# A hybrid decoder block on one core: operands three products ahead, residual loads among the merges, and three smaller moves

## The chip, the cores and the metric

The kernel runs on one core of a Trainium2 chip. TensorE (PE) multiplies, VectorE (DVE), ScalarE (ACT) and GpSimd (POOL) do the elementwise work, and SyncE (SP) issues most DMAs. The metric is the device time of one execution in microseconds (us); lower is better.

## The reference

One layer over 1024 tokens of width 1024, all in float32:

```
h = x + 1/2 * SwiGLU_1(rms(x))                      # hidden width 2816
u = rms(h);  [q | k | v | p | gate_logits] = u @ W_in
A: causal dilated window attention, 12 heads in 3 groups   -> @ W_A
B: causal means over 2/4/8/16 positions, 4 channel groups  -> @ W_B
h = h + (sigmoid(gA) * yA + sigmoid(gB) * yB) @ W_o
h = h + 1/2 * SwiGLU_2(rms(h))
out = rms_final(h)
```

## The kernel before

All products are in float32 split into two parts, a rounded high part and the rest, the lower part. A product of two such operands takes three matmuls (high times high, high times lower, lower times high; `three`). ScalarE makes the high part by a copy (L303), and VectorE or GpSimd makes the lower part by a subtraction (L306): VectorE for every third operand (`n_lo % 3`), GpSimd for the others.

The large products are done by a scheme of Strassen's kind with seven products instead of eight. In the projections a `Quad` is one block of 128 output columns with the products m = 1 to 7 in the order `ORDER = (1, 6, 2, 7, 5, 4, 3)`. Each is 12 matmuls of 128x512. `operand(m)` makes the weights' operand: for m = 6 it takes two sums on VectorE (L345, L347), for 7 and 3 one (L351, L356), and the rest take a piece or a sum that is there already. The operands lie in tiles of tag "wc", four of them. `run(m)` does the product into a PSUM bank; products 2 and 3 add onto the banks of 1 and 5. So the result of 5 (`out(5)`) has to be read before product 3 may begin. There are four PSUM banks of tag "mm" (products 1, 2, 5, 3) and four of tag "acc".

Most of the program is in stretches that are issued in the order in which they are written (`manual_schedule`): each engine takes its own instructions in that order and waits where one is not ready. These places matter here:

- `up` does the first half of a SwiGLU. For the column pairs that were begun early, a list `items` gives the products, and iteration k issues the operand of product k + 2, product k, and then the result of product k - 1 (`a_out`, `b_out`; L487 is `a_out(5)`).
- The input projection has 19 quads (`MIX`: three groups of q and k and of v, then pool and gate blocks) and does the same with `mix_operand`, `quad.run` and `Mix.out` (L982 to L999; L993 is `out(5)`). The first four quads have their products 1 and 2 done beforehand. The result of product 1 goes ahead of the operand. A list `later` holds jobs that go on by one step an iteration, behind the result: transposes of v (`turn`, L1058 to L1061), pool windows and their matmuls (`window`, L1078 to L1102), and `split_late`, which splits weights for later stages and stores them.
- The merges, 16 of them, come after attention. Merge k multiplies the attention parts (`att_parts`, four tiles of tag "h") with W_A into an "mm" bank (L1701), VectorE multiplies with the gate (L1703), GpSimd adds the pool branch (L1707), and SP is told to load the input of merge k + 5. The first eight do the first half of the tokens, the others the second; all of them read the four tiles of `att_parts`.
- The product with W_o goes by `step_o(i)`, i = 0 to 13, two steps for each of seven products; a step is four groups of six matmuls (`multiply_o`, L1884), one bank each. Products alternate between the "acc" and the "mm" banks. `sum_o` makes sums of merges on GpSimd, `split_o` the parts of the left operand (L1867 on ScalarE, `o_lo`, L1871, on VectorE), `load_whole` and `split_whole` the parts of single W_o blocks (L1381, L1408, L1411), `load_w_o` loads blocks that were split earlier (L1377), and `adds_o` adds a finished bank onto the residual h (L1890, L1892). `reload(t)` takes a new tile of tag "h" (there are eight) and loads the residual's rows of tile t into it (L1830), on SP's queue. Steps 0 and 1 stand among the merges.
- At the end `store_last` scales the last four row tiles and stores them; the last one goes in two halves on two queues.

A tile that is taken while all of its tag are in use makes the first instruction that writes it wait for the last reader of an old one; for a load this wait is at its place in the issuing engine's queue.

Of the kernel before, what the change touches and what calls it, by code (L numbers as in the profile page):

```python
# [13 lines left out]
OP = mybir.AluOpType  # L14
# [4 lines left out]
D = 1024  # L19
NT = S // P  # L20
# [98 lines left out]
def three(hi_lo_l, hi_lo_r):  # L119

    lh, ll = hi_lo_l
    rh, rl = hi_lo_r
    return ((lh, rh), (lh, rl), (ll, rh))
# [3 lines left out]
def tile_block(  # L127
# [28 lines left out]
    nc = tc.nc  # L156
# [31 lines left out]
    h = []  # L188
# [66 lines left out]
    inv = {}  # L255
# [10 lines left out]
    def scaled(t, out, gain):  # L266
        ve.scalar_tensor_tensor(out, h[t], inv.pop(t)[:, 1:2], gain, op0=OP.mult, op1=OP.mult)
# [119 lines left out]
    class Entry:  # L387
# [13 lines left out]
        def out(self, i):  # L401
            self.todo[i][2](self.todo[i][1], self.banks.pop(i))
# [152 lines left out]
    def up(sv, sums, between, name, room, begun):  # L555

        with tc.manual_schedule():
            last = ORDER[-1]  # L560
            items = [(q, w, m, out) for q in begun for w, out in ((q.A, q.a_out), (q.B, q.b_out))
                     for m in ORDER if m not in (1, 2)]
            then = Pair(sv, len(begun), sums)
            ahead = [(w, m) for _, w, m, _ in items] + [(then.A, m) for m in ORDER[:2]]
            parts, res = [], []
            for k, (q, w, m, out) in enumerate(items):
                ahead[k + 2][0].operand(ahead[k + 2][1])
                res.append(w.run(m))
                if m == last:
                    raws.depth = 6 if q is not begun[-1] else 4  # L570
                if k > 0:
                    p, _, m, out = items[k - 1]
                    out(m, res[k - 1])
                    for g in parts:
                        next(g, None)
                    if p is not q:
                        parts.append(p.parts())
            out = items[-1][3]
            out(last, res[-1])
            for g in parts:  # L580
                for _ in g:
                    pass
            begun[-1].finish()
        for j in range(len(begun), NPAIR - 1):
            q, then = then or Pair(sv, j, sums), None
            for m in ORDER:
                q.a(m)
            if j == NPAIR - 2:
                between()
            for m in ORDER[:-2]:  # L590
                q.b(m)
            if j == NPAIR - 2:
                end = Pair(sv, NPAIR - 1, sums)
                for m in ORDER[:2]:
                    end.A.operand(m)
            for m in ORDER[-2:]:
                q.b(m)
            q.finish()
        d = Down(name, sums, sv.half_tile, end)
        with tc.manual_schedule():  # L600
            items = [(w, m, out) for w, out in ((end.A, end.a_out), (end.B, end.b_out)) for m in ORDER]
            n = len(items)
            res = []
            for k, (w, m, out) in enumerate(items):
                if k + 2 < n:
                    items[k + 2][0].operand(items[k + 2][1])
                if k == 7:
                    d.load(0, tmp)
                    d.load(1, row)
                if k == n - 4:  # L610
                    d.sums_w(0)
                if k == n - 2:
                    raws.back(2)
                    d.sums_w(1)
                res.append(w.run(m, k < n - 1))
                if k == n - 1:
                    d.dp = room()
                    d.load(2)
                    d.begin(0)
                if k > 0:  # L620
                    items[k - 1][2](items[k - 1][1], res[k - 1])
            d.begin(1)
            end.b_out(ORDER[-1], res[-1])
        return d
# [583 lines left out]
    def mix_operand(k):  # L1208
        if k < len(items):
            q, m = items[k]  # L1210
            if q == len(mixes):
                mixes.append(Mix(svm, q))
            mixes[q].quad.operand(m, None if k > 1 else gp)
# [96 lines left out]
    with tc.manual_schedule():  # L1310
        entry.run(high_mix, after_mix)

        later, results = [], {}
        load_table(0)
        for k in range(len(items) + 4):
            if k - 1 in results and items[k - 1][1] == 1:
                mixes[items[k - 1][0]].out(1, results.pop(k - 1))
            mix_operand(k + 2)
            if k - 2 in range(len(items)):
                mixes[items[k - 2][0]].activate()  # L1320
            if k < len(items):
                q, m = items[k]
                results[k] = mixes[q].quad.run(m)
                if m == 7 and q < len(LATE):
                    later.append([k + 1, split_late(q)])
            if k - 1 in results:
                q, m = items[k - 1]
                mixes[q].out(m, results.pop(k - 1))
                if m == 3:
                    later.append([k, mixes[q].finish()])  # L1330
            for job in list(later):
                if job[0] <= k:
                    wait = next(job[1], 0)
                    job[0] = k + wait
                    if not wait:
                        later.remove(job)
            if k == 7 * 6:
                load_pool_w()
            if k == 7 * 12:
                tables.clear()  # L1340
                mask = keep.tile([P, 384], F32, tag="gain", bufs=1, name="mask")
                nc.sync.dma_start(mask, c_mask)
            if k == len(items) - 12:
                later.append([k, first_ring()])
            if k == len(items) - 7:
                load_pool(2)
                load_pool(3)
            if k == len(items) - 5:
                load_pool(0)
                load_pool(1)  # L1350
            if k == len(items) - 4:
                load_branch(0)
                load_values(0, row_part)
# [384 lines left out]
    with tc.manual_schedule():  # L1738
# [50 lines left out]
        q = N // 2  # L1789
# [83 lines left out]
    def split_o(i):  # L1873
        hi_o(i)
        lo_o(i)

    def multiply_o(i, t):
        m, st = divmod(i, 2)
        if m not in banks:
            banks[m] = [bank(("acc", "mm")[m % 2], f"wo{m}_{q}") for q in range(4)]  # L1880
        w, ts = w_o_parts[i], slice(t * P, (t + 1) * P)
        for j in range(2):
            for q, (l, r) in enumerate(three(tuple(v[:, j, ts] for v in ops[i]), tuple(w[:, v, j] for v in range(2)))):
                pe.matmul(banks[m][t], l, r, start=(st == 0 and j == 0 and q == 0), stop=(st == 1 and j == 1 and q == 2))  # L1884

    def add_o(m, t):
        for (th, n), sign in DOWN[m].to:
# [6 lines left out]
    def step_o(i, ts=range(4)):  # L1894
        for t in ts:
            multiply_o(i, t)
        if 3 in ts and (i + 3) // 2 in (2, 3, 4, 6) and i + 3 < STEPS:
            load_w_o(i + 3)

    def adds_o(m, ts):  # L1900
        for t in ts:
            add_o(m, t)
# [11 lines left out]
    with tc.manual_schedule():  # L1914
# [12 lines left out]
        for k in range(6, 11):  # L1927
            merge(k)
            if k in (7, 9):
                load_whole(2 + (k - 7) // 2)  # L1930
            if k == 8:
                sum_o(3)
                split_o(2)
        step_o(1)
        sum_o(4)
        split_o(3)
        for k in range(11, 16):
            merge(k)
            if k in (12, 14):
                split_whole(2 + (k - 12) // 2, ve)  # L1940
        for t in range(4, NT):
            reload(t)
        X2.update(sums_of_x(late["xa"], "f2", ("b21", "b11")))
        for i in range(2, STEPS - 4):
            step_o(i)
            m, st = i // 2 - 1, i % 2
            adds_o(m, range(2 * st, 2 * st + 2))
            if i in (6, 7):
                load_whole(i + 4)
            if i == 6:  # L1950
                ac.activation(warm, mhalf, AF.Silu)
            sum_o(i + 3)
            split_o(i + 2)
            if i in (8, 9):
                split_whole(i + 2, ve)

# [94 lines left out]
    def store_last(t):  # L2051
        rows = slice(t * P, (t + 1) * P)
        y = ends[t]
        if t < NT - 1:
            scaled(t, y, final_gain)
            nc.sync.dma_start(out[rows, :], y)
            return
        st = inv[t]
        ac.activation(y[:, LOWS], y[:, LOWS], AF.Copy, scale=st[:, 1:2])
        nc.scalar.dma_start(out[rows, LOWS], y[:, LOWS])  # L2060
        ve.scalar_tensor_tensor(y[:, HIGHS], h[t][:, HIGHS], st[:, 1:2], final_gain[:, HIGHS], op0=OP.mult, op1=OP.mult)
        nc.sync.dma_start(out[rows, HIGHS], y[:, HIGHS])
# [124 lines left out]
```

## Time and profile before

| | |
|---|---|
| median of 3 runs | 1917.43 us (1917.08 to 1917.56) |
| profiled execution | 1919.57 us |
| its span, first to last instruction | 1917.8 us |
| TensorE busy | 1900.8 us, 99% |
| VectorE busy | 1346.2 us, 70% |
| ScalarE, GpSimd busy | 760.0 and 733.5 us |
| granted TensorE clock | 0.999 |

A row of the waits reads: who waited, its line, for whom; us in total, number of times, the longest. A row of a timeline reads: start and duration in us, engine, line, operation, tile written <- tiles read, shapes, count, and in brackets the idle time before it and what ended it. PEld is TensorE's loading of weights, which overlaps its matmuls. In names of tiles, buffer numbers are left out: `u_mixm` is a bank of the input projection, `wc_mixm` an operand of it, `y_m` a result.

### The profile page before, as it was taken

Reading aid. Unit: us, or ns where it says so; the run is one execution under the profiler, and the core shown is the slowest. Engines: PE = TensorE matmul, PEld = TensorE weight load, DVE = VectorE, ACT = ScalarE, POOL = GpSimd, SP = SyncE. Lnnn points to the kernel's source line nnn. Section 1 sums busy time; section 2 is a strip of 40 time slices with the busy share of each in tenths; the row PEclk is TensorE's granted clock in tenths of the full one; section 3 lists DMA queues with packets and bytes.
Section 4 is the critical chain, followed back from the end, with each engine's and each line's share of the span. In section 5 each row is a group of like instructions: output and inputs, shape, how many; then the busy total and the mean of one; then the engine's idle time right before and its main releaser. Section 6 shows DMA issues by size and latency. Waiting matters only on the chain. (4 is left out here: it accounts for less than half of the span.)

```text
span 1917.8 us, 24914 instructions
## 1 busy us (share of the span) xinstructions
PE 1900.8 (99%) x8938; PEld 1575.5 (82%) x8938; DVE 1346.2 (70%) x2016; ACT 760.0 (40%) x1364; POOL 733.5 (38%) x548
## 2 busy tenths in 40 slices
PE   9999999999999999999999999999999999999998
PEld 7888888888888888888877888788888888888886
DVE  7886556657776776668875896788665556577777
ACT  6333333333344543334444762253333333333344
POOL 5433333331222365545544455553333333312132
PEclk9999999999999999999999999999999999999999
DMA  4154223336466627665567967643434223454564
GB/s 188 47 195 173 86 88 105 137 109 214 149 236 214 203 94 245 228 217 202 207 247 277 308 213 264 240 167 113 179 104 137 83 88 105 159 185 145 195 216 165
DMA packets 144796, 331.98 MB, mean 173 GB/s; under 512 B 19104, under 2 KB 39840, under 8 KB 143136
## 3 DMA queue, kind: packets, MB, share of 16 engines
q1 hardware_dynamic: 137136, 308.00, 46.1%
q10 hardware_dynamic: 7536, 22.39, 3.4%
q8 instruction: 70, 1.15, 0.2%
q14 instruction: 54, 0.44, 0.1%
HBM read 229.61 MB, written 100.73 MB: 172 GB/s over the span
## 5 line engine op out<-in xcount | busy, mean ns | idle before, releaser
L714 PE MATMUL d_f<-bhi_f,ahi_f 128*128 128x512 f32 x616 | 240.4, 390 | 0.0
L714 PE MATMUL d_f<-bhi_f,alo_f 128*128 128x512 f32 x616 | 239.7, 389 | 0.0
L714 PE MATMUL d_f<-blo_f,ahi_f 128*128 128x512 f32 x616 | 239.6, 389 | 0.0
L314 PE MATMUL u_mixm<-xhi_t_mix,wc_mixm 128*128 128x512 f32 x608 | 195.2, 391 | 1.1 <-POOL wc_mixm L306 1.0
L676 POOL TENSOR_TENSOR alo_f<-g_f,ahi_f 128x512 fp32r<-128x512 f32 x60 | 84.4, 1422 | 291.8 <-ACT ahi_f L672 291.8
L314 PE MATMUL u_mixm<-xhi_b_mix,wc_mixm 128*128 128x512 f32 x456 | 149.0, 392 | 0.3 <-DVE y_m L993 0.3
L714 PEld LDWEIGHTS d_f<-bhi_f,alo_f 128*128 128x128 f32 x616 | 115.6, 188 | 24.1
L714 PEld LDWEIGHTS d_f<-bhi_f,ahi_f 128*128 128x128 f32 x616 | 115.6, 188 | 24.0 <-DVE xlo_b_mix L385 0.2
L314 PEld LDWEIGHTS u_mixm<-xhi_t_mix,wc_mixm 128*128 128x128 f32 x608 | 113.8, 188 | 26.2 <-POOL wc_mixm L306 2.7
L714 PEld LDWEIGHTS d_f<-blo_f,ahi_f 128*128 128x128 f32 x616 | 115.7, 188 | 23.8
L314 PE MATMUL u_mixm<-xlo_t_mix,wc_mixm 128*128 128x512 f32 x304 | 118.4, 389 | 0.0
L306 POOL TENSOR_TENSOR wc_mixm<-s_mixm,wc_mixm 128x512 fp32r<-128x512 f32 x52 | 74.0, 1425 | 100.4 <-ACT wc_mixm L303 96.4
L314 PEld LDWEIGHTS u_mixm<-xhi_b_mix,wc_mixm 128*128 128x128 f32 x456 | 85.6, 188 | 18.3 <-issue 0.7
L303 ACT ACTIVATE wc_mixm<-s_mixm 128x512 fp32r<-128x512 f32 x76 | 47.5, 629 | 126.7 <-DVE s_mixm L347 67.4
L314 PE MATMUL u_mixm<-xlo_b_mix,wc_mixm 128*128 128x512 f32 x228 | 88.8, 389 | 0.0
L672 ACT ACTIVATE ahi_f<-g_f 128x1024 fp32r<-128x1024 f32 x84 | 81.9, 975 | 3.6 <-DMA g_f<-gs_f 3.6
L306 POOL TENSOR_TENSOR wc_mixm<-raw,wc_mixm 128x512 fp32r<-128x512 f32 x40 | 60.6, 1519 | 45.0 <-ACT wc_mixm L303 38.1
L672 ACT ACTIVATE bhi_f<-s_f2w 128x512 fp32r<-128x512 f32 x55 | 32.7, 627 | 94.4 <-DVE s_f2w L692 84.3
L1884 PE MATMUL wo<-w_o,o_hi 128*128 128x512 f32 x224 | 69.5, 391 | 0.2 <-issue 0.2
L314 PEld LDWEIGHTS u_mixm<-xlo_t_mix,wc_mixm 128*128 128x128 f32 x304 | 57.1, 188 | 11.7
L672 ACT ACTIVATE bhi_f<-s_f1w 128x512 fp32r<-128x512 f32 x55 | 32.9, 630 | 82.7 <-DVE s_f1w L692 77.8
L676 DVE TENSOR_TENSOR alo_f<-g_f,ahi_f 128x1024 fp32r<-128x1024 f32 (+1 forms) x48 | 58.7, 1223 | 7.7 <-ACT ahi_f L672 7.7
(1312 smaller groups left out, 5106.7 us busy)
## 6 DMA issues: line engine op xcount, KB each, us to landing
g_f<-gs_f SPq DMA_DIRECT2D x70, 512.0 KB, 4.7
gs_f<-y_f SPq DMA_DIRECT2D x88, 256.0 KB, 2.9
raw<-in_w2a_dram SPq DMA_DIRECT2D x35, 512.0 KB, 3.3
raw<-in_w2b_dram SPq DMA_DIRECT2D x35, 512.0 KB, 3.3
gs_f<-gb_f SPq DMA_DIRECT2D x46, 256.0 KB, 2.3
raw<-in_w1a_dram SPq DMA_DIRECT2D x22, 512.0 KB, 5.6
raw<-in_w3a_dram SPq DMA_DIRECT2D x22, 512.0 KB, 5.6
raw<-in_w1b_dram SPq DMA_DIRECT2D x22, 512.0 KB, 4.2
```

Source lines behind the costliest of these rows:

```text
L303: ac.activation(w[:, 0], src, AF.Copy)
L306: eng.tensor_tensor(w[:, 1], src, w[:, 0].bitcast(F32), op=OP.subtract)
L314: pe.matmul(p, a, b, start=(start and k == 0 and q == 0), stop=(k == 3 and q == 2), skip_group_check=not start)
L672: ac.activation(hi[:, c], src, AF.Copy)
L676: eng.tensor_tensor(lo[:, d], src[:, o], hi[:, d].bitcast(F32), op=OP.subtract)
L714: pe.matmul(self.banks[m][t], l, r, start=(first and q == 0), stop=(last and q == 2))
L1884: pe.matmul(banks[m][t], l, r, start=(st == 0 and j == 0 and q == 0), stop=(st == 1 and j == 1 and q == 2))
```

## The change

Five edits. The fifth result is issued ahead of the operand in `up`. In the input projection the operand of product k + 3 instead of k + 2 is issued in iteration k, and `split_late` begins one iteration earlier. In `multiply_o` the matmuls with the lower part of the left operand come last of the six. `reload(4)` and `reload(5)` move from behind the merges to behind merges 8 and 9, and at i = 2 `split_o(4)` moves ahead of the adds. The last store but one is scaled and stored in two halves.

```diff
@@ up
             for k, (q, w, m, out) in enumerate(items):
+                soon = k > 0 and items[k - 1][2] == 5
+                if soon:
+                    items[k - 1][3](5, res[k - 1])
                 ahead[k + 2][0].operand(ahead[k + 2][1])
...
                     p, _, m, out = items[k - 1]
-                    out(m, res[k - 1])
+                    if not soon:
+                        out(m, res[k - 1])
@@ the input projection's loop
-            mix_operand(k + 2)
+            if k == 0:
+                mix_operand(2)
+            mix_operand(k + 3)
...
                 if m == 7 and q < len(LATE):
-                    later.append([k + 1, split_late(q)])
+                    later.append([k, split_late(q)])
@@ multiply_o
-        for j in range(2):
-            for q, (l, r) in enumerate(three(tuple(v[:, j, ts] for v in ops[i]), tuple(w[:, v, j] for v in range(2)))):
-                pe.matmul(banks[m][t], l, r, start=(st == 0 and j == 0 and q == 0), stop=(st == 1 and j == 1 and q == 2))
+        for n, (q, j) in enumerate((q, j) for qs in ((0, 1), (2,)) for j in range(2) for q in qs):
+            l, r = three(tuple(v[:, j, ts] for v in ops[i]), tuple(w[:, v, j] for v in range(2)))[q]
+            pe.matmul(banks[m][t], l, r, start=(st == 0 and n == 0), stop=(st == 1 and n == 5))
@@ the merges and steps
             if k == 8:
                 sum_o(3)
                 split_o(2)
+                reload(4)
+            if k == 9:
+                reload(5)
...
-        for t in range(4, NT):
+        for t in range(6, NT):
             reload(t)
...
             m, st = i // 2 - 1, i % 2
+            if i == 2:
+                split_o(i + 2)
             adds_o(m, range(2 * st, 2 * st + 2))
...
             sum_o(i + 3)
-            split_o(i + 2)
+            if i > 2:
+                split_o(i + 2)
@@ store_last
         if t < NT - 1:
-            scaled(t, y, final_gain)
-            nc.sync.dma_start(out[rows, :], y)
+            st = inv.pop(t)
+            for c in (LOWS, HIGHS) if t == NT - 2 else (slice(0, D),):
+                ve.scalar_tensor_tensor(y[:, c], h[t][:, c], st[:, 1:2], final_gain[:, c], op0=OP.mult, op1=OP.mult)
+                nc.sync.dma_start(out[rows, c], y[:, c])
             return
```

## The prediction

> **What bounds the kernel now.** I read the page's busy shares first, then the waits of TensorE (the matmuls' and the weight loads') by stretches, then the timelines of the places that they name.
>
> ```profile
> PE 1900.8 (99%) x8938; PEld 1575.5 (82%) x8938; DVE 1346.2 (70%) x2016; ACT 760.0 (40%) x1364; POOL 733.5 (38%) x548
> PE wo L1884 <- DVE o_lo L1871: 1.9, 2, 1.7
> PE u_mixm L314 <- POOL wc_mixm L306: 1.0, 2, 0.6
> PE u_f21a L314 <- DVE y_f L487: 0.5, 1, 0.5
> PEld u_mixm L314 <- POOL wc_mixm L306: 2.7, 4, 1.1
> PEld wo L1884 <- DVE o_lo L1871: 2.8, 2, 2.1
> ```
>
> TensorE is busy for 1900.8 of 1917.8 us, so nothing that another engine does counts unless a matmul waits for it. The change alters neither the number nor the shape of the matmuls. What it can win is the few waits listed; what it can lose is any new wait. All working below is therefore a list of waits of TensorE, gone and new. The matmul rows undercount a wait, since the modelled end of a matmul overruns the start of the next; the weight-load rows overcount it a little. One place calibrates both:
>
> ```profile
> 1193.02 6.96 PE L1701 MATMUL ya<-att,ya 128*128 128x512 f32 x30
> 1211.07 0.70 PE L1884 MATMUL wo<-w_o,o_hi 128*128 128x512 f32 x2 [0.15 <-issue]
> 1213.44 0.50 PE L1884 MATMUL wo<-w_o,o_lo 128*128 128x512 f32 x1 [1.67 <-DVE o_lo L1871]
> ```
>
> Thirty matmuls in 6.96 us, the last one 0.39 long, start every (6.96 - 0.39) / 29 = 0.227 us. Two matmuls from 1211.07 make the third due at 1211.52; it started at 1213.44, so 1.92 us were lost where one row says 1.67 and the other 2.1. I add 0.25 to a matmul row or take 0.2 from a weight-load row.
>
> **Waits that the change removes.** The fifth result first (`up`): m = 3 adds onto the bank of m = 5, so it waits until `a_out(5)` (L487) has read that bank. VectorE reaches that read behind the operand of the product after next:
>
> ```profile
> 1338.15 0.68 DVE L345 TENSOR_TENSOR s_f21b<-raw 128x512 f32<-128x512 f32 x1
> 1338.87 0.69 DVE L347 TENSOR_TENSOR s_f21b<-s_f21b,raw 128x512 f32<-128x512 f32 x1
> 1339.67 0.63 ACT L303 ACTIVATE wc_f21b<-s_f21b 128x512 fp32r<-128x512 f32 x1 [3.36 <-DVE s_f21b L347]
> 1340.34 0.69 DVE L306 TENSOR_TENSOR wc_f21b<-s_f21b,wc_f21b 128x512 fp32r<-128x512 f32 x1 [0.78 <-ACT wc_f21b L303]
> 1340.95 0.68 DVE L487 TENSOR_TENSOR y_f<-u_f21a,y_f 128x512 f32<-128x512 f32 x1
> 1341.78 0.47 PE L314 MATMUL u_f21a<-xhi_b_f,wc_f21a 128*128 128x512 f32 x1 [0.52 <-DVE y_f L487]
> ```
>
> Moved ahead of the two sums, the read no longer waits for them: 0.52 + 0.25 = 0.75 us gone. The operand comes 0.7 us later and has a whole product (12 x 0.227 = 2.72 us) to spare. The other started pairs show no such wait, so nothing is counted for them.
>
> Operands three ahead: the four waits for a lower part by GpSimd sum to 2.7 - 4 x 0.2 = 1.9 us, bounds 1.0 and 2.7. A lead of one more product covers the longest (1.1), so I count 1.9 us gone.
>
> Lower parts last, and `split_o(4)` ahead of the adds: the two waits for `o_lo` are 2.8 - 2 x 0.2 = 2.4 us, and the pair at 1211.07 started 0.3 after it was due (its bank was still being added, below). The low parts are now wanted two matmuls (0.45 us) later, and at i = 2 they no longer stand behind three adds. I count 2.7 us gone, bounds 1.9 and 3.3.
>
> The last store but one by halves:
>
> ```profile
> 1911.33 1.28 DVE L267 SCALAR_TENSOR_TENSOR hn_n<-h_last,nst,gain_final 128x1024 f32<-128x1024 f32 x1
> 1913.06 0.75 DVE L2061 SCALAR_TENSOR_TENSOR hn_last<-h_last,nst_last,gain_final 128x512 f32<-128x512 f32 x1 [0.44 <-POOL nst_last L2088]
> ```
>
> Its first half is ready after about 0.7 us instead of 1.28, so its transfer starts some 0.6 us earlier and is out of the way of the very last one. Two halves cost VectorE 0.2 us more, inside the 0.44 that L2061 waits anyway. Between 0 and 0.6; I take 0.3. Sum removed: 0.75 + 1.9 + 2.7 + 0.3 = 5.65 us.
>
> **What operands three ahead add.** In iteration k the operand of product k + 3 now stands ahead of the result of k - 1. Where k - 1 is the fifth product of a quad, k + 3 is the sixth of the next quad (the order is 1, 6, 2, 7, 5, 4, 3): the operand with two sums, L345 and L347. That is just the order which cost `up` its wait, and `Mix.out(5)` (L993) is not moved ahead here. Each third operand gets its lower part from VectorE (`n_lo % 3`); counted through the list, the sixth is among them for the quads after 3, 6, 9, 12 and 15 (behind quads 0 to 2 the sums fall a product earlier, since the next quad has only five products left). Where VectorE is free, the sums run while product five is still on TensorE and cost nothing: over the run it is busy 70% of the time. But in some quads a job of the iteration before holds VectorE until after product five has ended, by waiting for transposes or pool matmuls that TensorE does behind product five. These are its rows for the fifth result, and the third product's start:
>
> ```profile
> 803.23 0.69 DVE L1061 TENSOR_TENSOR v<-tv,v 128x512 fp32r<-128x512 f32 x1 [3.10 <-ACT v L1060]
> 744.29 0.68 DVE L993 TENSOR_TENSOR y_m<-u_mixm,y_m 128x512 f32<-128x512 f32 x1
> 745.61 0.39 PE L314 MATMUL u_mixm<-xhi_b_mix,wc_mixm 128*128 128x512 f32 x1
> 803.83 0.68 DVE L993 TENSOR_TENSOR y_m<-u_mixm,y_m 128x512 f32<-128x512 f32 x1
> 805.52 0.48 PE L314 MATMUL u_mixm<-xhi_b_mix,wc_mixm 128*128 128x512 f32 x1
> 862.89 0.68 DVE L993 TENSOR_TENSOR y_m<-u_mixm,y_m 128x512 f32<-128x512 f32 x1
> 864.58 0.48 PE L314 MATMUL u_mixm<-xhi_b_mix,wc_mixm 128*128 128x512 f32 x1
> 923.00 0.68 DVE L993 TENSOR_TENSOR y_m<-u_mixm,y_m 128x512 f32<-128x512 f32 x1
> 924.75 0.39 PE L314 MATMUL u_mixm<-xhi_b_mix,wc_mixm 128*128 128x512 f32 x1
> 962.44 0.68 DVE L993 TENSOR_TENSOR y_m<-u_mixm,y_m 128x512 f32<-128x512 f32 x1
> 964.19 0.39 PE L314 MATMUL u_mixm<-xhi_b_mix,wc_mixm 128*128 128x512 f32 x1
> 1004.06 0.68 DVE L306 TENSOR_TENSOR wc_mixm<-raw,wc_mixm 128x512 fp32r<-128x512 f32 x1
> 1005.48 0.47 PE L314 MATMUL u_mixm<-xhi_b_mix,wc_mixm 128*128 128x512 f32 x1 [0.32 <-DVE y_m L993]
> ```
>
> They are quads 3, 6, 9, 12, 14 and 16; the first row is the job that held VectorE in quad 6, and L993 began as it ended. In `up` the stretch from the start of the first sum to the start of the third product is 1341.78 - 1338.15 = 3.63 us. Put where L993 begins now, it makes the third product start at 747.92, 807.46, 866.52 and 926.63: 2.31, 1.94, 1.94 and 1.88 us late, 8.1 in all. Where GpSimd makes the lower part, the stretch is two sums and the read, 1.41 + 0.83 = 2.24 us: quad 14 would start it at 962.44 + 2.24 = 964.68, 0.5 late, and quad 16, where L306 moves ahead and the sums take its place, at 1004.06 + 2.24 = 1006.30, 0.8 late. New waits: 9.4 us. From below: none, if the sums get in ahead of the job; from above 3 more, if a weight load that the first sum needs is not there a product earlier. I take 9.4, as each term comes from a row of the same order of the same instructions.
>
> [...]
>
> **What the residual loads add.** `reload` takes a tile of tag "h", of which there are 8. Beside merge 8 all are in use: four hold `att_parts`, which every merge to the last reads, and four hold h[0] to h[3]. So `reload(4)` waits for a tile that TensorE gives back only in merge 15, and it waits at the head of SP's queue, ahead of the loads of merge 14, of `load_whole(3)` and of merge 15:
>
> ```profile
> 1192.95 0.32 SPq L1686 DMA_DIRECT2D merge<-gate  x1
> 1195.22 0.38 SPq L1381 DMA_DIRECT2D w_o_in<-in_w_o_dram  x1
> 1199.95 0.32 SPq L1686 DMA_DIRECT2D merge<-gate  x1
> 1201.31 2.08 SPq L1830 DMA_DIRECT2D h_again<-h_dram  x4
> 1199.72 1.06 ACT L1408 ACTIVATE w_o<-w_o_in 128x1024 fp32r<-128x1024 f32 x1 [2.91 <-DMA w_o_in<-in_w_o_dram]
> 1200.82 1.44 DVE L1411 TENSOR_TENSOR w_o<-w_o_in,w_o 128x1024 fp32r<-128x1024 f32 x1 [0.85 <-ACT w_o L1408]
> 1203.10 0.69 DVE L1703 TENSOR_TENSOR merge<-merge,ya 128x512 f32<-128x512 f32 x1 [0.85 <-DMA merge<-gate]
> 1203.90 0.44 PE L1884 MATMUL wo<-w_o,o_hi 128*128 128x512 f32 x1
> 1210.28 1.29 DVE L1890 TENSOR_TENSOR h_again<-wo,h_again 128x512 f32<-128x512 f32 x2 [5.89 <-DMA h_again<-h_dram]
> GB/s 0 0 0 49 82 115 229 221 311 385 344 320 393 287 377 262 393 393 328 393 393 393 328 393 377 344 426 377 426 410 426 393 426 442 377 442 410 410 442 393
> ```
>
> Merge 15 ends at 1193.02 + 6.96 = 1199.98; the first tile is free after its second matmul, about 1199.3. From there SP issues reload(4), merge 14, whole(3), reload(5), merge 15, 0.5 MB each. The GB/s row (0.25 us a slice from 1199.95, a queue that had run dry) moves 1.05 MB in 4.5 us, 1.57 in 5.9 and 2.62 in 8.5. So merge 14 lands at 1203.8, whole(3) at 1205.2, merge 15 at 1207.8. TensorE does not need these loads for the merges, but the third and the fourth product of `step_o(2)` take over the "mm" banks of merges 14 and 15, and the fourth started at 1203.90, right behind merge 15's multiply (1203.10 + 0.69). VectorE's new order: merge 14 to 1204.5, the lower part of w_o(3) to 1205.2 + 1.06 + 1.44 = 1207.7, merge 15 to 1208.5. The fourth product starts at 1208.6, 4.7 us late. Landings can lag the bytes: reload(4), behind 1.5 MB, would by this row have landed 7.1 us after 1199.95 and was there at 1210.28, 3.2 us more. Bounds 4.7 and 7.9; I take 5.2, near the lower one, since VectorE took the multiply at 1203.10 just as the row has its bytes done (0.55 MB). With that, reload(4) is long there when the adds come.
>
> [...]
>
> **Sum.** -5.65 + 9.4 + 5.2 = +9.0 us. The profiled execution took 1919.57 us (span 1917.8, and 1.8 around it) and would take 1928.6; the median of the runs, 1917.43, lies 2.1 below it, and on it the sum is 1926.4 us. By itself this case runs from 1921.5 (only half of the projection's terms) to 1930.
>
> **Rivals.** (a) Faster: the written order does not bind, because the framework's queues let the reload and the operands stand where they hold up nothing. Then all is gain, 1917.43 - 5.65 = 1911.8. It decides if the fifth result stays within 1.0 us of where it was in quads 6, 9 and 12 and SP does not stop after merge 13. For it: the slack of the fifth result is above 1 us in most quads. Against: L993 behind L1061 and L487 behind L306 are in the written order. (b) The sums get in ahead of the held job, and only SP's stop costs: -5.65 + 5.2 = -0.45, 1917.0. Against: the job is written into the iteration before. (c) A tile is free for reload(4) and only the projection pays: -5.65 + 9.4, 1921.2. Against: 4 + 4 tiles of 8. (d) Worse: landings lag by 3.2 us, and weights come late for the sums: +2.7 + 3, about 1932.
>
> **How the numbers follow.** The main case has 0.66, (a) 0.11, (b) 0.10, (c) 0.08, (d) 0.05. A measurement of this kernel can tell about 0.2%, 3.8 us, from no change: (a) is faster; (b), (c) and a little of the main case are the same; the rest is slower. The range 1916.5 to 1930.5 leaves out (a) and (d), 0.16.
>
> **What would show it.** Right: the matmul waits for `u_mixm` on L993's successor rise from 0.3 to some 9 us in about six places, with the sums ahead of it on VectorE; the waits for GpSimd's lower parts, for `o_lo` and for L487 are gone; SP issues nothing between merge 13's load and the end of merge 15; TensorE waits some 5 us for merge 14 and 15's multiplies within `step_o(2)`. Wrong: no new wait for the fifth result in quads 3, 6, 9 and 12, or merge 14's load issued before merge 15's matmuls.

## The result, and the profile after

| | before | after |
|---|---|---|
| median of 4 runs | 1917.38 us (1917.08 to 1917.56) | 1943.33 us (1941.49 to 1946.3) |
| ratio, 95% interval | | 1.0134 [1.0122, 1.0146] |
| profiled execution, its span | 1919.57, 1917.8 us | 1946.3, 1944.5 us |
| granted TensorE clock | 0.999 | 0.993 |

The change costs 26 us, where 9.0 were forecast; 1943.33 lies outside the range 1916.5 to 1930.5. The side was right, the size was nearly three times too small. The page's busy shares and the waits of TensorE's matmuls and weight loads after the change:

```profile
PE 1910.4 (98%) x8938; PEld 1582.1 (81%) x8938; DVE 1327.7 (68%) x2017; ACT 761.5 (39%) x1364; POOL 731.3 (38%) x548
```

```profile
PE u_mixm L314 <- DVE y_m L998: 13.7, 7, 3.2
PE wo L1892 <- DVE merge L1710: 6.3, 2, 4.1
PEld u_mixm L314 <- ACT wc_mixm L303: 11.3, 4, 3.6
PEld wo L1892 <- DVE merge L1710: 7.4, 2, 4.5
```

(Behind `up`, the lines of the changed kernel are 5 or more higher: the fifth result L993 is L998, the merge's multiply L1703 is L1710.) The waits for GpSimd's lower parts, for `o_lo` and for L487 are gone but for 0.2 us, as forecast. Two new ones stand there, both of the kind that was forecast and for the most part in the places. They are 20.0 us. (The row of L303, 11.3, is the same wait seen from the weight load. Ahead of quad 3's third product that copy, of another product's operand, had ended at 748.76, the read L998 ended at 749.26, and the load began at 749.37.) Span and page show two more things. PE's busy time rose by 9.6 us with the same 8938 matmuls, and the granted clock fell. The third product of quad 3 shows why, in rows of TensorE:

```profile
745.85 0.39 PE L314 MATMUL u_mixm<-xhi_t_mix,wc_mixm 128*128 128x512 f32 x1
749.40 0.77 PE L314 MATMUL u_mixm<-xhi_b_mix,wc_mixm 128*128 128x512 f32 x1 [3.17 <-DVE y_m L998]
749.97 0.63 PE L314 MATMUL u_mixm<-xlo_b_mix,wc_mixm 128*128 128x512 f32 x1
750.39 1.05 PE L314 MATMUL u_mixm<-xhi_b_mix,wc_mixm 128*128 128x512 f32 x2
754.24 0.63 PE L314 MATMUL u_mixm<-xhi_b_mix,wc_mixm 128*128 128x512 f32 x1
755.64 0.40 PE L314 MATMUL u_mixm<-xlo_b_mix,wc_mixm 128*128 128x512 f32 x1
```

After 3.3 us without a matmul the next ones start 0.43 us apart (750.39 - 749.97 = 0.42) and take 0.63 instead of 0.40: TensorE runs at half its rate from 748.45 to 755.28 (granted clock 0.50 in the row below), and then as before (0.40 again at 755.64). Busy time by stretches, with the granted clock behind the busy times (the third number from the right):

```profile
745.04:748.45 3.41, 1.19 (x6) 0.65 (x4) 2.62 (x3) 1.15 (x3) 1.69 (x1) 1.00 0.59 230
748.45:755.28 6.83, 5.88 (x15) 4.64 (x16) 4.05 (x7) 0.31 (x1) 3.72 (x3) 0.50 0.48 190
813.30:816.72 3.42, 1.56 (x7) 1.33 (x8) 3.00 (x5) 1.69 (x4) 1.98 (x2) 1.00 0.54 208
874.75:878.16 3.41, 1.45 (x6) 1.23 (x7) 2.89 (x5) 2.01 (x4) 1.84 (x2) 1.00 0.56 220
878.16:881.57 3.41, 3.41 (x9) 2.67 (x8) 2.28 (x3) 0.55 (x2) 1.13 (x1) 0.50 0.34 136
1001.04:1004.45 3.41, 1.52 (x8) 1.09 (x7) 2.72 (x4) 2.30 (x4) 1.44 (x2) 1.00 0.24 94
1004.45:1007.86 3.41, 3.41 (x10) 2.63 (x9) 3.14 (x5) 0.23 (x1) 1.12 (x1) 0.50 0.00 0
1222.90:1226.32 3.42, 0.50 (x2) 0.46 (x3) 0.69 (x1) 0.00 (x0) 0.40 (x1) 1.00 0.87 292
1226.32:1236.56 10.24, 8.03 (x19) 5.77 (x19) 7.98 (x12) 3.07 (x3) 6.86 (x6) 0.50 1.02 406
```

The stretches at half rate are 6.83, 3.41, 3.41 and 10.24 us long: two, one, one and three times 3.41. Their starts lie whole multiples of 3.413 apart (748.45, 878.16, 1004.45, 1226.32: 38, 75 and 140 of them from the first). So in this execution the clock changed only on a grid of 3.413 us, and the window before each stretch holds TensorE's wait: it stood still there for 2.22, 1.96, 1.89 and 2.92 us (length less the first busy time).

Matching the n-th matmul of one trace with the n-th of the other shows where the 26.7 us of span came from: third products late 15.6, half rate behind them 6.0, GpSimd's lower parts -1.8; in `step_o(2)` waits 6.9 and half rate 3.5, then `o_lo` -2.4; `up` -0.7; a drift of -0.3 elsewhere (rounded, so the sum is 0.1 off).

### The profile page after: what moved, and what is told of

It reads as the page before. It is cut to its first block, busy times and chain, and to the rows that moved or that the text cites. A ratio compares the mean times of both kernels' runs of the same rounds, so it can differ in the third digit from the quotient of the medians.

```text
span 1944.5 us, 24892 instructions
## 1 busy us (share of the span) xinstructions
PE 1910.4 (98%) x8938; PEld 1582.1 (81%) x8938; DVE 1327.7 (68%) x2017; ACT 761.5 (39%) x1364; POOL 731.3 (38%) x548
## 5 line engine op out<-in xcount | busy, mean ns | idle before, releaser
L314 PE MATMUL u_mixm<-xhi_b_mix,wc_mixm 128*128 128x512 f32 x456 | 153.8, 404 | 14.3 <-DVE y_m L998 13.7
L314 PEld LDWEIGHTS u_mixm<-xhi_b_mix,wc_mixm 128*128 128x128 f32 x456 | 88.1, 193 | 36.0 <-ACT wc_mixm L303 11.3
L303 ACT ACTIVATE wc_mixm<-s_mixm 128x512 fp32r<-128x512 f32 x76 | 47.9, 630 | 142.5 <-DVE s_mixm L347 53.0
L1892 PE MATMUL wo<-w_o,o_hi 128*128 128x512 f32 x224 | 63.0, 405 | 6.3 <-DVE merge L1710 6.3
L314 PEld LDWEIGHTS u_mixm<-xlo_t_mix,wc_mixm 128*128 128x128 f32 x304 | 57.1, 188 | 11.7
```

The lines of the kernel that those rows point to most:

```text
L303: ac.activation(w[:, 0], src, AF.Copy)
L314: pe.matmul(p, a, b, start=(start and k == 0 and q == 0), stop=(k == 3 and q == 2), skip_group_check=not start)
L1892: pe.matmul(banks[m][t], l, r, start=(st == 0 and n == 0), stop=(st == 1 and n == 5))
```

## The experiments

My theory after the result: the two new waits of the prediction, larger than forecast, and each made dearer by the clock that halves behind it. The rivals: the waits alone (the half rate has another cause); one place causes all; the jobs of `split_late`, which the change starts one iteration earlier, are what holds VectorE.

**Undoing one part each (e1, e2) and both (e3).**

```
e1:  -            if k == 0: mix_operand(2)        e2:  -                reload(4)   (behind merge 8)
     -            mix_operand(k + 3)                    -                reload(5)   (behind merge 9)
     +            mix_operand(k + 2)                    -        for t in range(6, NT): reload(t)
     -  later.append([k, split_late(q)])                +        for t in range(4, NT): reload(t)
     +  later.append([k + 1, split_late(q)])       e3:  both
```

> The changed kernel with the input projection put back (operands two products ahead, split_late one iteration later); everything else of the change stays. Theory (waits and clock): the projection holds 15.7 us of waits for the fifth result and 5.7 us of matmuls at half rate behind them, less 1.8 won on lower parts, 19.4 us net by the shift between the two traces; without it 1943.3 - 19.4 = 1923.9 us, clock losses left only in step_o(2). Rival (waits alone: the half-rate matmuls have some other cause and stay): 1943.3 - 13.7 = 1929.6. Rival (one place causes all, the loads): near 1940.

> The changed kernel with reload(4) and reload(5) put back behind the merges. Theory: the two waits in step_o(2) (4.25 and 2.61 us) and the half-rate matmuls behind them (3.5 us) go, 10.3 us: 1933.0. Rival (waits alone): 6.9 us, 1936.4, with half-rate matmuls left near step_o(2). Rival (the wait comes from the new order of the lower parts, not from SP's queue): 1943.

> Only the fifth result first, the lower parts last with split_o(4) ahead, and the last store by halves. By the shift between the two traces these win 0.3 + 0.65 (fifth result), 2.06 + 0.36 (lower parts): 3.4 us, so 1917.4 - 3.4 = 1914.0, granted clock 0.999. By the sum of the prediction 0.75 + 2.7 + 0.3 = 3.75: 1913.7. Rival (the small edits win nothing by themselves): 1917.4.

Measured: e1 1923.42 us (ratio to before 1.0028 [1.0017, 1.0038]), e2 1937.08 (1.0102 [1.0087, 1.0117]), e3 1915.89 (0.9990 [0.9981, 0.9999]). No one place causes all: against e3, the projection's edit costs 1937.08 - 1915.89 = 21.2 us and the reloads 7.5. "Waits alone" forecast 1929.6 for e1 and falls. e2 missed its theory, 1933.0, and lies at the figure of "waits alone", 1936.4. Its trace has full clock all through `step_o(2)` (1.00 from 1210 to 1260), though, and is 11.0 us shorter than that of the change, where 10.3 were expected. But the 10.3 came from the slowest execution of the change, 3.0 above its median. e3 won about half of what was expected (more on this in the next section). The profiled execution of e1 (1921.38) had both waits of `step_o(2)` and no half rate beside them (clock 1.00 from 1195 to 1240):

```profile
PE wo L1890 <- DVE merge L1708: 5.1, 2, 2.9
```

```profile
1204.36 1.20 PE L1890 MATMUL wo<-w_o,o_hi 128*128 128x512 f32 x4 [2.20 <-DVE merge L1708]
1208.89 1.20 PE L1890 MATMUL wo<-w_o,o_hi 128*128 128x512 f32 x4 [2.88 <-DVE merge L1708]
```

Its four matmuls take 1.20 us, where the trace of the change has 1.67 and 2.08. So waits at the same two places were followed by half rate in one execution and not in the other; of the other seven runs of e1, six (1922.9 to 1923.8) showed a granted clock of 0.998 and one (1925.10) 0.996, where the profiled one showed 0.999. In e2 the grid lies elsewhere: the first stretch at half rate in its trace begins 2.22 us later than in that of the change, which is no whole window:

```profile
750.67:754.08 3.41, 3.41 (x10) 2.63 (x9) 2.80 (x4) 0.00 (x0) 2.91 (x3) 0.50 0.77 306
```

I take that for one reason why the runs of e1 and of the change spread (by 3.7 and 4.8 us): in both the slowest run has the lowest clock, 0.996 and 0.993. It is not the only one: the first trace of the kernel before shows no half rate ahead of the end, and 18 runs of it, all at 0.999, reach from 1917.0 to 1920.3.

**The reload's place in the queue (e8).** e1 with the two reloads behind merge 10, which issues the last of the merges' loads:

```
             if k == 8:
...
-                reload(4)
-            if k == 9:
-                reload(5)
+            if k == 10:
+                reload(4)
+                reload(5)
```

> As run e1 (projection put back), but reload(4) and reload(5) stand behind merge 10, whose load of merge 15 is the last of the merges' loads, instead of behind merges 8 and 9. Theory: the reload's wait for a tile now holds up nothing on SP's queue, and the 5.5 us of waits in step_o(2) go: 1916 as in run e3. Rival (the reload's bytes or its tile are what the merges wait for, not the queue): 1923.

Measured: 1915.59 us, 0.9991 [0.9983, 1.0], and no wait for a merge. The tiles and the bytes are the same; only the place on SP's queue differs. In e8 merge 15's load goes out first, and the reload behind it:

```profile
1198.77 0.32 SPq L1691 DMA_DIRECT2D merge<-gate  x1
1199.66 0.86 SPq L1835 DMA_DIRECT2D h_again<-h_dram  x2
```

That step of the prediction is shown. In the changed kernel SP's rows are the forecast ones:

```profile
1208.76 0.32 SPq L1694 DMA_DIRECT2D merge<-by_pool  x1
1218.14 0.32 SPq L1837 DMA_DIRECT2D h_again<-h_dram  x1
1218.55 1.30 SPq L1693 DMA_DIRECT2D merge<-gate  x1
1219.90 0.42 SPq L1694 DMA_DIRECT2D merge<-by_pool  x1
1225.07 0.69 DVE L1710 TENSOR_TENSOR merge<-merge,ya 128x512 f32<-128x512 f32 x1 [7.10 <-DMA merge<-gate]
1229.81 0.69 DVE L1710 TENSOR_TENSOR merge<-merge,ya 128x512 f32<-128x512 f32 x1 [0.34 <-DMA merge<-gate]
```

Nothing is issued from 1208.76 to 1218.14, the reload goes first, and the multiplies of merges 14 and 15 come at 1225.07 and 1229.81, 6.9 and 11.7 us after 1218.14.

**Is it the standing still that halves the clock? (e5)** Eight matmuls that nobody reads fill a part of the wait, in the changed kernel:

```
+                if m == 3 and q in (3, 6, 9, 12, 15):
+                    p, x = bank('acc', f'fill{q}'), X_mix['b11'][0]
+                    for n in range(8):
+                        pe.matmul(p, x[:, n % 4, :P], x[:, n % 4], start=True, stop=True)
                 results[k] = mixes[q].quad.run(m)
```

> The changed kernel with eight extra matmuls (1.8 us, into a bank that nobody reads, from operands that are long there) on TensorE ahead of the third product of quads 3, 6, 9, 12 and 15, which wait 2 to 3.4 us there. Theory (the clock halves because TensorE stands still in these waits): the third products start when they did, but no half-rate stretch follows in the projection: 5.7 us less by the trace, about 1937.6, and the granted clock there is 1.00. Rival (the half rate has another cause, such as the traffic in those stretches): the stretches stay, 1943 or a little more. Rival (the extra matmuls come late and hold up the product): 1945 or more.

Measured: 1940.6 us (1.0121 [1.0106, 1.0137]). The same three places, by stretches of e5:

```profile
745.00:757.00 12.00, 10.56 (x51) 8.46 (x50) 9.79 (x14) 3.15 (x7) 6.72 (x6) 1.00 0.58 224
872.00:885.00 13.00, 12.57 (x58) 10.13 (x57) 9.06 (x14) 5.06 (x9) 5.58 (x5) 1.00 0.52 198
1000.00:1012.00 12.00, 11.94 (x53) 9.60 (x52) 9.47 (x13) 4.99 (x9) 7.02 (x5) 1.00 0.35 129
```

```profile
750.16 0.47 PE L314 MATMUL u_mixm<-xhi_b_mix,wc_mixm 128*128 128x512 f32 x1 [1.44 <-DVE y_m L998]
```

The third product starts at 750.16, 3.64 us after product five's last matmul began, where it was 3.55 (745.85 to 749.40), and the clock stays at 1.00 in all three places. The profiled execution gained 6.7 us on that of the change (1939.56 against 1946.3), the median only 2.7 of the 5.7 expected: the change's profiled run was the slowest of its four, and the four runs of each overlap (1937.7 to 1942.8, 1941.5 to 1946.3). So the times alone do not decide. The trace does, for its own execution: in `step_o(2)`, where nothing fills the waits (4.2 us in two places), the mean clock from 1215 to 1235 is 0.74, and in the three places that were filled it is 1.00. In this kernel, then, the half rate comes with TensorE's standing still.

**The jobs of `split_late` (e6).** Their steps after the first go on one iteration later again:

```
         flat = [raws.get() for _ in pieces]
-        yield 1
+        yield 2
```

> The changed kernel with the jobs of split_late going on one iteration later after their first step (the pieces are still taken in the same order). Theory: its VectorE sums (L1140 of the changed kernel, 0.68 to 1.77 us) no longer stand ahead of the sixth operand's sums in quads 9, 10, 12, 14 and 15: 0.6 + 0.65 + 0.6 + 0.5 + 1.8 = 4.1 us less, and one half-rate stretch (1.4) less: 1938 to 1939. Rival (the sums of the operand alone make the wait): 1943. Rival (these jobs are the main cause): below 1930.

Measured: 1943.01 us, no gain. The third products of quads 9, 10, 12 and 14 came about 0.6 us less late, as expected, and quad 6 1.1. But quad 15, of which 1.8 was expected, is 2.14 late after 2.05; quad 11 now waits 1.96, which it had not, and quad 3 4.18 instead of 3.33 (the transposes of `turn` held VectorE longer there). In quads 11 and 15 the first of the two sums now waits for its weights:

```profile
DVE s_mixm L345 <- DMA raw<-in_w_pin_dram: 3.7, 1, 3.7
DVE s_mixm L345 <- DMA raw<-in_w_gb_dram: 1.1, 1, 1.1
```

These loads take over tiles that, among others, the jobs of `split_late` give back when they are done. So the jobs make 0.6 to 1.1 us of the lateness of five quads, but one iteration later two quads get their weights late. As the main cause they are out: quads 6, 9 and 12 are still 1.8 us late.

**The fifth result first in the projection (e4), a fifth operand tile (e7).** e2 with the order that `up` got:

```
-            if k - 1 in results and items[k - 1][1] == 1:
-                mixes[items[k - 1][0]].out(1, results.pop(k - 1))
+            if k - 1 in results and items[k - 1][1] in (1, 5):
+                q, m = items[k - 1]
+                mixes[q].out(m, results.pop(k - 1))
e7, besides, in `split`, with `more` a tile of the tag "y" that is free from quad 3 on:
+            if self.more is not None and self.turn % 5 == 0:
+                w = self.more
```

> The changed kernel with the reloads put back and, in the projection, the fifth result issued ahead of the operand as the first one is, operands still three ahead. Theory: the waits for the fifth result and the half-rate stretches go while the 1.8 us won on GpSimd's lower parts stays: 1914.0 - 1.8 = 1912.2. Rival (early splits: the jobs of split_late, one iteration earlier, are what holds VectorE): waits of about 0.6 us stay in five quads, about 1915. Rival (late operands): the sixth operand, now behind the fifth result, makes its own product late, about 1917.

> The kernel with the fifth result first in the projection and the reloads back (run e4, 1925.0), with a fifth operand tile from quad 3 on. Theory: the 9 us that it lost against expectation come from the four operand tiles: an operand three ahead takes the tile of the product before the running one, so ScalarE stands at its head until TensorE has ended that product (57.0 us in 32 waits in the changed kernel, 7.2 in 7 before), and all that is queued behind on ScalarE, the stores and loads of the rotation and the first results among it, comes late. With the fifth tile these waits fall below 15 us, the 4.8 us wait for the first result of quad 4 goes: 1912 to 1916. Rival (the order behind the two sums, not the tile): 1925.

Measured: e4 1925.04 us (1.0036 [1.0024, 1.0049]), 12 us better than e2 and 13 worse than I expected; e7 1924.65, the same. The wait for the fifth result fell from 13.7 us to 1.3, and another took its place:

```profile
PE u_mixm L314 <- ACT y_m L987: 7.8, 4, 4.8
PE u_mixm L314 <- DVE y_m L998: 1.3, 1, 1.3
```

```profile
752.32 0.75 DVE L1043 STREAM_SHUFFLE ro<-ro 128x512 f32<-128x512 f32 x1
756.69 1.15 DVE L351 TENSOR_TENSOR s_mixm<-raw,raw 128x512 f32<-128x512 f32 x1
757.93 0.63 ACT L303 ACTIVATE wc_mixm<-s_mixm 128x512 fp32r<-128x512 f32 x1 [8.44 <-DVE s_mixm L351]
758.94 0.59 ACT L987 ACTIVATE y_m<-u_mixm 128x512 f32<-128x512 f32 x1
```

L987 is the first result, on ScalarE; product 2 adds onto its bank. It stands behind L303, the copy of the operand three ahead: the seventh product's, whose sum (L351) waits on VectorE behind the rotation's shuffle. With operands two ahead the copy there was the second product's, which takes no sum. (The shuffle had waited 3.9 us for its load.) The operand tiles looked guilty: ScalarE's waits for TensorE to give one back were 57.0 us in 32 places after the change, 7.2 in 7 before. In e4 they are 22.8, in e7 10.9, and the time is the same, so in this order they cost TensorE nothing that can be told from 0.

**Both results ahead of the sums (e9), with five tiles (e10).** e4, and where the first product runs, the operand of k + 3 is issued an iteration later, behind the first result:

```
+            first = k < len(items) and items[k][1] == 1
+            if 0 < k <= len(items) and items[k - 1][1] == 1:
+                mix_operand(k + 2)
+            if not first:
                 mix_operand(k + 3)
```

> Run e4 (fifth result first in the projection, reloads back, 1925.0) with one operand less ahead at one place of each quad: the seventh product's operand (one sum on VectorE) is issued an iteration later, behind the first result instead of ahead of it. Theory (the same fault on a second queue: on ScalarE the first result stood behind the copy of an operand whose sum waited on VectorE behind the rotation): the waits for the first result (7.8 us in 4 places) and the half-rate stretch go, and the 1.8 us of GpSimd's lower parts stay won: about 1914. Rival (the rotation's loads alone are late, wherever the operand stands): 1920 to 1925.

> Run e9 with a fifth operand tile from quad 3 on. Theory: with both results ahead of the sums, ScalarE's wait for an operand tile is covered, and the tile is worth less than 1 us: 1913 to 1914.5. Rival (with the order mended the four tiles are the next limit): 2 us or more below e9.

Measured: e9 1918.55 us (1916.83 to 1922.62; 1.0003 [0.9995, 1.0012]), e10 1917.82 (0.9999 [0.9990, 1.0008]). The wait for the first result is gone and 6.5 us are won, so the second queue is shown. But 1914 was not reached: operands three ahead stay 2 to 3 us worse than two (e3), also with the order mended. The fifth tile is worth under 1 us, as expected. In the profiled execution of e9 (1917.07), 1.5 us of waits for the fifth result are left in three places; what makes other executions of it up to 5.5 us longer stays open.

**The kernel before once more (e11).**

> The kernel before, profiled once more. The prediction took its removed waits from an execution of 1919.6 us, 2.1 above the median of the runs. Theory: part of those waits (2.8 us for o_lo, 2.7 for GpSimd's lower parts) belonged to that execution: an execution near 1917.4 shows less than half of one of the two. Rival (they are in every execution, and the 2.1 us lies elsewhere): both within 0.5 us of what they were.

The second profiled execution took 1917.69 us. Its waits of TensorE's weight loads:

```profile
PEld u_mixm L314 <- POOL wc_mixm L306: 3.0, 5, 1.1
PEld wo L1884 <- DVE o_lo L1871: 0.7, 1, 0.7
```

The lower parts by GpSimd are in every execution; of `o_lo`'s two waits only 0.7 is left of 2.8, and against the first trace the matmuls lie 1.74 us earlier from just that place (1211.70 for 1213.44) to the end.

## Why the prediction was wrong, step by step

| step of the sum | forecast | measured |
|---|---|---|
| fifth result first in `up` | -0.75 | -0.65 (e3: -0.77) |
| GpSimd's lower parts | -1.9 | -1.8 |
| lower parts last, `split_o(4)` | -2.7 | -2.4 in the traces, 1.7 of it one execution's |
| last store by halves | -0.3 | +0.1 (last matmul's start to the end: 7.62 in both traces of before, 7.68 to 7.93 in the eleven with the edit) |
| third products late | +9.4 | +15.6 |
| half rate behind them | 0 | +6.0 |
| merges 14 and 15 late | +5.2 | +6.9 (e1: 5.5) |
| half rate behind them | 0 | +3.5 (e1: 0) |

**Right:** what bounds the kernel, the two places, the order on VectorE, SP's stop at reload(4), the bounds of 4.7 and 7.9 for it (7.5 by the medians), and two of the four gains. Rivals (a), (b) and (c) are excluded by e1 and e2: each of two edits costs by itself. Of (d), the late landings came: the multiplies of merges 14 and 15 began 6.9 and 11.7 us after the reload's issue (5.1 and 9.6 in e1), where the bytes had given 4.5 and 8.5. The late weights did not, in the trace of the change.

**The term that failed most is "What operands three ahead add":** 7.5 us net forecast, 21.2 measured. Three things were missed in it.

First, the clock. The working took a wait of TensorE for its own length and put the half rate behind it at nothing, without a reason. In the trace of the change that held for the shorter ones (up to 1.86 us of standing still in a window of 3.41); behind the four windows with 1.89 to 2.92 came half rate, 6.0 + 3.5 us. The trace of before could not show it: its only half rate lies behind the last matmul.

Second, the rows of one quad were taken as fixed lengths. They were 2.31, 1.94, 1.94 and 1.88 us late by forecast for quads 3, 6, 9 and 12, and 3.33, 2.96, 2.43 and 2.36 by trace. Quad 3, VectorE and GpSimd:

```profile
743.66 1.30 POOL L306 TENSOR_TENSOR wc_mixm<-raw,wc_mixm 128x512 fp32r<-128x512 f32 x1 [2.88 <-ACT wc_mixm L303]
744.93 1.79 POOL L1146 TENSOR_TENSOR raw<-raw,late_hi 128x512 fp32r<-128x512 f32 x1
744.90 0.68 DVE L345 TENSOR_TENSOR s_mixm<-raw 128x512 f32<-128x512 f32 x1
745.67 1.60 DVE L347 TENSOR_TENSOR s_mixm<-s_mixm,raw 128x512 f32<-128x512 f32 x1
747.97 0.69 DVE L306 TENSOR_TENSOR wc_mixm<-s_mixm,wc_mixm 128x512 fp32r<-128x512 f32 x1 [0.69 <-ACT wc_mixm L303]
748.58 0.68 DVE L998 TENSOR_TENSOR y_m<-u_mixm,y_m 128x512 f32<-128x512 f32 x1
```

The order is the forecast one: both sums, the lower part, then the fifth result. But L347 took 1.60, not 0.69, beside GpSimd's L1146, a step of `split_late`; quad 6 had the same with L345. In e6, where GpSimd's steps lie elsewhere, the same sums take 0.69 and 0.68 (below: quad 6 in the change, then quads 3 and 6 in e6):

```profile
810.43 1.80 DVE L345 TENSOR_TENSOR s_mixm<-raw 128x512 f32<-128x512 f32 x1
810.39 1.30 POOL L1146 TENSOR_TENSOR raw<-raw,late_hi 128x512 fp32r<-128x512 f32 x1 [1.84 <-ACT late_hi L1145]
747.46 0.69 DVE L347 TENSOR_TENSOR s_mixm<-s_mixm,raw 128x512 f32<-128x512 f32 x1
810.91 0.68 DVE L345 TENSOR_TENSOR s_mixm<-raw 128x512 f32<-128x512 f32 x1
```

In quad 9 a sum of `split_late` stood ahead of the pair:

```profile
872.51 0.68 DVE L1140 TENSOR_TENSOR raw<-raw,raw 128x512 f32<-128x512 f32 x1
873.11 0.68 DVE L345 TENSOR_TENSOR s_mixm<-raw 128x512 f32<-128x512 f32 x1
```

That was the part of the change whose cost I never wrote down: `split_late` one iteration earlier. It puts its sums and its GpSimd steps where the operand's sums now are. With the jobs back (e6), quads 6, 9 and 12 are 1.83, 1.83 and 1.76 late, close to the forecast, so there the rows were priced rightly for the operand alone, and quad 10 (0.65 late) is in time. Quads 0 (0.7) and 15 (2.05) were not in the forecast either, and stay late in e6. In quad 0 an operand with one sum (L351) and VectorE's lower part stands ahead of the fifth result. Quad 15 stands in the prediction's list of lower parts on VectorE, but not among its rows; its two sums began late, behind a sum of `split_late` in the change and behind their weights in e6. Quad 14 was 0.97 late (forecast 0.5), and quad 16 not at all (0.8).

Third, the bound from above, "3 more", was worked out for one mishap (late weights) and held neither of these. That mishap came in e6 alone.

**The store by halves** gained nothing. Its first half was ready after 0.75 us instead of 1.28, as forecast. But GpSimd's last step on the way (L2088), beside which VectorE now scales the second half, took 0.72 instead of 0.59, and the last scalings began 3.03 us after the last matmul's start instead of 2.90.

**A smaller fault** lies in going from the profiled execution to the median: I took `o_lo`'s waits off as a gain, and then also the 2.1 us by which the execution was slower than the median. e11 shows that 1.7 us of the waits were that excess. On medians the three edits that e3 holds won 1.6 us, not 3.75.

The fastest kernels here are e3 and e8, the change without its projection part and with the reloads behind the merges' loads: 1915.9 and 1915.6 us, about 0.1% below before.

## What to carry to other kernels

When an operand is fetched a step earlier, list for every engine which result now stands behind it: here both results on which a bank's reuse hangs had stood behind operands that need no sum, and one step more put sums ahead of each, on two engines. List as well what else the change starts earlier on those engines. A load that must wait for its tile belongs behind the last load that need not (1923.42 us in e1, 1915.59 in e8). In the trace of the change the windows of 3.41 us in which TensorE stood still for up to 1.86 us had no half rate behind them; the four with more had seven windows at half rate, which cost 6.0 us (four of them) and 3.5 us (three), and in e1's profiled execution waits of 2.20 and 2.88 us had none. So bound such a wait from above with the half rate that can follow it: here one to three windows, each by my estimate at most half of 3.41 us, 1.7; and before a wait of one profiled execution is counted as a gain, look whether a second one has it.

## What the hardware showed that I had not expected

**The clock.** In the trace of the change the windows of 3.41 us at full clock in which TensorE stood still for 1.89, 1.96, 2.22 and 2.92 us were followed by half rate, and in the middle of the kernel none with 1.86 or less was: 1004.45 followed 3.41 - 1.52 = 1.89, and 813.30 to 816.72 with 3.42 - 1.56 = 1.86 had no effect. In e2 the window ahead of 750.67 has 3.41 - 0.68 = 2.73:

```profile
747.26:750.67 3.41, 0.68 (x3) 0.62 (x4) 2.22 (x5) 1.46 (x3) 0.05 (x1) 1.00 0.56 208
```

One gap of 2.28 us between two starts was enough (1000.89 to 1003.17, nearly all in one window), and two of 2.59 and 3.27 in e1 were not; where a grid lay in e1 is not shown. In the trace of the change a window at half rate was the last of its stretch when TensorE stood still in it for 0.00 us (4 cases), and not when it did for 0.82 to 1.39 (3 cases). So the first stretch here has two windows: the wait reached 0.95 us into it (748.45 to 749.40).

**Sums on VectorE beside GpSimd.** Of the 38 sums L345 and L347 in the trace of before, 30 took 0.69 us on average and had GpSimd busy beside them for 0.01 us on average; 8 took 1.18 to 1.80 and had it beside them for 0.6 to 1.8. In quad 3 of the change, L1146 ends at 746.72 (744.93 + 1.79) and L347 0.55 later, as if it had begun only then; L345 of quad 3, which began 0.03 us ahead of L1146, took 0.68. e6 took GpSimd's steps away from two of those sums, which fell to 0.69 and 0.68. What lengthens a sum beside GpSimd is not shown by any run.
